# State-space weights prepared in the feed-forward block, full 128x128 output products, and attention steps that alternate with one step of other work

## The chip, the cores and the metric

The kernel runs on one core of a Trainium2 chip. The metric is the device time of one execution in microseconds (us), the median of several runs. The engines are TensorE (PE), VectorE (DVE), ScalarE (ACT), GpSimd (POOL) and SyncE (SP); SP only issues DMAs here. TensorE's granted clock is shown as a share of full speed: 1.00 is 2.4 GHz, 0.50 is 1.2 GHz.

## The reference

A sequence of 512 tokens of width 1024 goes through two layers of a first block (latent and differential attention) and then through two layers of a second block, to which the change belongs. A layer of the second block is a gated feed-forward block, a token mixer and another feed-forward block:

```
x = post_add(x, swiglu(pre(x, 0), ffn_w_in[l, 0], ffn_w_out[l, 0]), 0, 0.5)
y = token_mixer(pre(x, 1), ...)
x = post_add(x, y, 1, 1.0)
x = post_add(x, swiglu(pre(x, 2), ffn_w_in[l, 1], ffn_w_out[l, 1]), 2, 0.5)
```

The mixer projects its input to u, q, k, v, f and two gates, and computes

```
state[t] = lam_bar * state[t-1] + b_bar u[t]       (complex, 32 groups x 64 states)
y_ssm    = Re(C state) + d u                       (512 wide)
y_a      = z_val * sigmoid(z_gate),  z = gelu(y_ssm) @ glu_w
y_b      = forgetting_attention(q, k, v, f) @ attn_w_out      (causal, 8 heads)
out      = (sigmoid(g_a) y_a + sigmoid(g_b) y_b) @ w_out
```

lam_bar, b_bar and the powers of lam_bar depend on parameters alone, not on x.

## The kernel before, in words

Every large product is done as three matmuls on a high and a low part of both sides (`mm3`, L336 to L338; for products with tokens on the output's rows, `tokens`, L413 to L415). Weights stream in 512 KB units (`unit`): SP loads raw, ScalarE casts the high part (L319), VectorE subtracts to get the low part (L320); there are three buffers of each. A weight block (`mblock`) is 24 matmuls of 512 columns into one PSUM tile `acc`. The program is written in Python generators; a scheduler then puts the instructions in an order for each engine's queue, and each queue runs strictly in its order.

`ffn` works through 22 pairs of gate and up columns in chunks of SPLIT_K = 8, 7, 7. For a pair there are two weight blocks, then L1053 (tanh), L1054 and L1055 (products on VectorE), and a split into high and low (L425 on ScalarE, L428 on VectorE or GpSimd by turns). `pairs` opens a chunk's buffers by touching each on GpSimd (L396). After a chunk the four token tiles are multiplied with the chunk's output weights. Between, `pump` runs steps of the modulation (L999, one load and one VectorE operation each). After the first chunk of a layer's first feed-forward block, `ssm_params` computes lam_bar's powers.

`mixer` projects u and q, sends u through DRAM to get a layout by groups (four groups q of 128 channels), and runs three generators side by side: `ssm`, the attention (`fox_in`, `fox`), and the gated products. `side` interleaves them by the table MIX. For each q, `ssm` loads 256 KB of B and C, forms b_bar times powers on VectorE (`cplx`, L1223 to L1228), transposes it (L1248), forms C times powers and a rotation table on GpSimd (L1218 to L1263 and again L1223 to L1228), then the convolution kernel inside blocks of four tokens (L1278, L1281, masked at L1284), the inputs to the states (L1292), a scan on VectorE (L1303) and the outputs: four products of decreasing width (L1323) and 32 narrow ones with 32 weight columns (L1328), followed by a gelu. The attention's `fox` handles 8 heads; a head has scores for its query tiles (L575), masks, exponentials (L601), transposes (L584) and products with v (L1521).

Of the kernel before, what the change touches and what calls it, by code (L numbers as in the profile page):

```python
# [10 lines left out]
F32 = mybir.dt.float32  # L11
# [14 lines left out]
SPLIT_K = (8, 7, 7)  # L26
NH = 6
MIX = (1, 3, 1, 16)
# [5 lines left out]
BUFS = dict(raw=3, wh=3, wl=3, big=34, tmp=5, hf=3, ms=5, s16=8, pw=1, pr=1, acc=3, att=2, aux=2, yps=1, mod=2, sums=1)  # L34
# [114 lines left out]
def make_consts():  # L149
# [7 lines left out]
    c[:, C_BLK:C_BLK + 128] = (q // 32 == k // 32).astype(f)  # L157
# [79 lines left out]
class Net:  # L237
# [804 lines left out]
    def ffn(self, l, i, h, nxt, between):  # L1042
# [3 lines left out]
        for p, n in enumerate(SPLIT_K):  # L1046
# [24 lines left out]
            if p < len(SPLIT_K) - 1:  # L1071
                for t in range(4):
# [22 lines left out]
    def ssm_params(self, l):  # L1095
# [38 lines left out]
        v.scalar_tensor_tensor(ab, in0=th, scalar=-1.0, in1=th, op0=ALU.mult, op1=ALU.max)  # L1134

# [58 lines left out]
        v.tensor_tensor(wi, wi, d1, op=ALU.mult)  # L1194
        for j in range(3):
# [7 lines left out]
        return dict(rho=r[:, 3], tc=tc_, ts=ts_, l=(lr, li), f=(fr, fi))  # L1203

    def ssm(self, l, P, u, ud, out):

        nc = self.nc
        v, g = nc.vector, nc.gpsimd
        d4 = [128, 4, 4, 32]

        def v4(t):
            return t.rearrange("p (a b c) -> p a b c", a=4, b=4)

        def v3(t):
            return t.rearrange("p (a b) -> p a b", a=4)

        def mul(o, a, b):
            g.tensor_tensor(o, a, b, op=ALU.mult)  # L1218

        def cplx(e, o, a, b, c, d, view):  # L1220

            t = self.big()
            e.tensor_tensor(view(o[:, 0]), a, c, op=ALU.mult)  # L1223
            e.tensor_tensor(view(t[:, 0]), b, d, op=ALU.mult)
            e.tensor_tensor(o[:, 0], o[:, 0], t[:, 0], op=ALU.subtract)
            e.tensor_tensor(view(o[:, 1]), a, d, op=ALU.mult)
            e.tensor_tensor(view(t[:, 1]), b, c, op=ALU.mult)
            e.tensor_tensor(o[:, 1], o[:, 1], t[:, 1], op=ALU.add)  # L1228

        for q in range(4):  # L1230
            pq = slice(q * 4, q * 4 + 4)
            bk = self.big()
            bc, kt = v3(bk[:, 0]), v3(bk[:, 1])
            nc.sync.dma_start(bk[:, 0], self.io["ssmbc"][l, q])
            bl = self.big()
            b0, b1 = (v3(bk[:, 0])[:, c].rearrange("p (a b) -> p a b", a=4).unsqueeze(2).to_broadcast(d4)
                      for c in range(2))
            f0, f1 = (f[:, pq].unsqueeze(3).to_broadcast(d4) for f in P["f"])
            cplx(v, bl, b0, b1, f0, f1, v4)
            bb = self.tmp(256)  # L1240
            nc.scalar.copy(bb.rearrange("p (c a b) -> p c a b", c=2, a=4),
                           bl.rearrange("p c (a j b) -> p c a j b", a=4, j=4)[:, :, :, 3])
            gt = self.big()
# [9 lines left out]
            nc.scalar.mul(bc[:, 3], bc[:, 3], -1.0)  # L1253
            cl = self.big()
            cv = [bc[:, c].rearrange("p (a b) -> p a b", a=4).unsqueeze(1).to_broadcast(d4) for c in (2, 3)]
# [326 lines left out]
```

## Time and profile before

| | |
|---|---|
| median of 3 runs | 3258.07 us (3257.98 to 3263.37) |
| profiled execution | 3255.93 us, span 3254.2 us, granted clock 0.99 |
| TensorE busy | 97% of the span |
| VectorE, ScalarE, GpSimd busy | 59%, 37%, 16% |
| DMA | 385.8 MB, mean 119 GB/s |
| stages of the second block | 935, 1308, 1720, 2094, 2466, 2882 us to the end |

The stages were read from the stores of the residual at each stage's end: from 935 us the first feed-forward block of layer 0, then its mixer, its second feed-forward block, and the same three for layer 1. "Busy" counts instructions in work, not peak use; a matmul's recorded end is modelled and overlaps the next one's start, so that prices of matmuls are taken from distances between starts. Idle time of an engine is listed with the instruction whose end released it.

### The profile page before, as it was taken

To read this page: it belongs to the slowest core of one execution; us is meant where nothing else is said; L and a number is where in the kernel's file an instruction comes from. 1 tells how busy PE (TensorE), PEld (TensorE's weight loads), DVE (VectorE), ACT (ScalarE), POOL (GpSimd) and SP (SyncE) were. 2 spreads that over 40 slices of the span, in tenths; PEclk is the share of its full clock that TensorE was granted. 3 is DMA by queue.
4 is the path that set the end of the run, shared out by engine and by line. 5 is a ranking of instruction groups with operands and counts; after the bars stand their busy time and mean duration, and the time that the engine had idled before them with its cause. 6 is when DMAs were issued, how large, how long until landed. Compare 5 with 4: busy or idle time off the path is not lost. (4 is left out here: it accounts for less than half of the span.)

```text
span 3254.2 us, 42296 instructions
## 1 busy us (share of the span) xinstructions
PE 3150.2 (97%) x16138; PEld 2568.7 (79%) x16138; DVE 1932.3 (59%) x3517; ACT 1208.1 (37%) x2103; POOL 513.2 (16%) x580
## 2 busy tenths in 40 slices
PE   8999999999999999998999999999998989999999
PEld 8777878778788888876778888888888777788887
DVE  4787765787855847567565533634345676653334
ACT  3455433555332313334443222432234434442312
POOL 1200132000230101353001000100003340010000
PEclk9999999999999999999999999999999999999999
DMA  5242532243626537321233632332233221322313
GB/s 170 95 146 89 181 142 86 89 140 109 215 89 209 199 114 250 98 84 53 72 123 104 201 104 95 139 110 81 95 136 108 72 69 52 124 98 97 128 66 110
DMA packets 135514, 385.80 MB, mean 119 GB/s; under 512 B 15840, under 2 KB 22544, under 8 KB 135312
## 3 DMA queue, kind: packets, MB, share of 16 engines
q1 hardware_dynamic: 132208, 377.31, 34.3%
q0 software_dynamic: 1056, 3.17, 0.3%
q10 hardware_dynamic: 2048, 2.62, 0.3%
q8 instruction: 127, 2.08, 0.3%
q14 instruction: 75, 0.61, 0.1%
HBM read 361.52 MB, written 18.90 MB: 117 GB/s over the span
## 5 line engine op out<-in xcount | busy, mean ns | idle before, releaser
L336 PE MATMUL acc<-big,wh 128*128 128x512 f32 (+1 forms) x2744 | 1068.4, 390 | 13.2 <-DVE tmp L719 8.5
L337 PE MATMUL acc<-big,wh 128*128 128x512 f32 (+1 forms) x2744 | 1062.2, 387 | 0.7 <-POOL big L513 0.7
L338 PE MATMUL acc<-big,wl 128*128 128x512 f32 (+1 forms) x2744 | 1060.9, 387 | 0.0
L320 DVE TENSOR_TENSOR wl<-raw,wh 128x1024 fp32r<-128x1024 f32 x394 | 500.9, 1273 | 539.7 <-ACT wh L319 515.2
L319 ACT CAST wh<-raw 128x1024 fp32r<-128x1024 f32 x394 | 413.4, 1049 | 1001.2 <-PE acc L337 490.8
L336 PEld LDWEIGHTS acc<-big,wh 128*128 128x128 f32 x2744 | 520.1, 190 | 124.0 <-issue 10.2
L338 PEld LDWEIGHTS acc<-big,wl 128*128 128x128 f32 x2744 | 519.7, 189 | 106.4 <-issue 0.6
L337 PEld LDWEIGHTS acc<-big,wh 128*128 128x128 f32 x2744 | 520.5, 190 | 103.2 <-POOL big L513 1.2
L999 DVE SCALAR_TENSOR_TENSOR ms<-ms,big 128x512 f32<-128x512 f32 x288 | 198.7, 715 | 48.9 <-DMA ms<-in_modw_dram 48.4
L428 POOL TENSOR_TENSOR big<-tmp,big 128x512 fp32r<-128x512 f32 (+1 forms) x44 | 70.0, 1591 | 810.5 <-ACT big L425 810.5
L1055 DVE SCALAR_TENSOR_TENSOR tmp<-tmp,acc 128x512 f32<-128x512 f32 (+1 forms) x88 | 57.1, 649 | 150.5 <-PE acc L338 150.2
L425 ACT ACTIVATE big<-tmp 128x512 fp32r<-128x512 f32 (+1 forms) x148 | 88.0, 595 | 145.2 <-POOL tmp L875 58.0
L320 DVE TENSOR_TENSOR big<-raw,big 128x1024 fp32r<-128x1024 f32 x92 | 114.8, 1259 | 14.0 <-ACT big L319 14.0
L413 PE MATMUL acc<-big,big 128*128 128x512 f32 x288 | 112.9, 392 | 0.0
L415 PE MATMUL acc<-big,big 128*128 128x512 f32 x288 | 112.5, 391 | 0.0
L415 PE MATMUL att<-big,big 128*128 128x512 f32 x288 | 112.4, 390 | 0.0
L414 PE MATMUL acc<-big,big 128*128 128x512 f32 x288 | 112.4, 391 | 0.0
L413 PE MATMUL att<-big,big 128*128 128x512 f32 x288 | 112.2, 390 | 0.0
L414 PE MATMUL att<-big,big 128*128 128x512 f32 x288 | 112.2, 389 | 0.0
L319 ACT CAST big<-raw 128x1024 fp32r<-128x1024 f32 x92 | 94.7, 1042 | 43.7 <-DMA raw<-in_w_dram 43.7
L601 ACT ACTIVATE big<-att,sm 128x512 f32<-128x512 f32 (+2 forms) x112 | 69.5, 623 | 110.0 <-DVE sm L599 98.9
L584 PE MATMUL aux<-cst,big 128*128 128x128 f32 x512 | 95.3, 284 | 12.9 <-DVE big L589 5.5
(399 smaller groups left out, 5014.0 us busy)
## 6 DMA issues: line engine op xcount, KB each, us to landing
raw<-in_w_dram SPq DMA_DIRECT2D x486, 512.0 KB
ms<-in_modw_dram SPq DMA_DIRECT2D x288, 256.0 KB
xb2l0s<-big SPq DMA_DIRECT2D x12, 512.0 KB
big<-xb2l0s SPq DMA_DIRECT2D x12, 512.0 KB
xb1l<-big SPq DMA_DIRECT2D x8, 512.0 KB
big<-xb1l SPq DMA_DIRECT2D x8, 512.0 KB
xb2l1s<-big SPq DMA_DIRECT2D x8, 512.0 KB
big<-xb2l1s SPq DMA_DIRECT2D x8, 512.0 KB
```

What stands on the lines that cost most here:

```text
L319: nc.scalar.copy(hi[:, :n], raw[:, :n])
L320: nc.vector.tensor_tensor(lo[:, :n], raw[:, :n], hi[:, :n].bitcast(F32), op=ALU.subtract)
L336: nc.tensor.matmul(ps, lhsT=hi, rhs=a, start=first, stop=False)
L337: nc.tensor.matmul(ps, lhsT=hi, rhs=b, start=False, stop=False)
L338: nc.tensor.matmul(ps, lhsT=lo, rhs=a, start=False, stop=last)
L413: nc.tensor.matmul(ps[m], lhsT=a, rhs=hi, start=c == o[0], stop=False)
L414: nc.tensor.matmul(ps[m], lhsT=a, rhs=lo, start=False, stop=False)
L415: nc.tensor.matmul(ps[m], lhsT=b, rhs=hi, start=False, stop=c == o[-1])
L425: nc.scalar.activation(hi, src, AF.Copy, scale=scale)
L428: eng.tensor_tensor(lo, src, hi.bitcast(F32), op=ALU.subtract)
L584: nc.tensor.transpose(ps[:, j * 128:(j + 1) * 128], p[:, kc * 128:(kc + 1) * 128], self.ident)
L999: nc.vector.scalar_tensor_tensor(w, in0=w, scalar=0.5, in1=self.sc[m], op0=ALU.mult, op1=ALU.mult, accum_out=sums[:, n, m:m + 1])
```

## The change

A new generator `ssm_prep` does in a layer's first feed-forward block what depends on parameters alone. It is advanced by one step at each weight block and each output token tile. First come the parameters in five steps, then for each q the complex products, now all on VectorE (new L1229 to L1231, 18 operations a group), the transposes (new L1268), and the convolution kernel as 16 narrow products (new L1287, L1290). GpSimd's queue stores four 512 KB tiles for each q in DRAM (new L1235, L1304 to L1308; the zeros of the triangular tile too). This block's chunks become 5, 5, 5, 7, and it pumps half as many modulation steps; these run in later blocks instead. In the mixer, `ssm` loads the four tiles and u one group ahead on SP. The outputs are 128x128 products (new L1376, L1378) and go through DRAM on GpSimd's queue to get back to their layout. `side` and its table go; each of 24 attention steps is followed by one gate block or gated product (`fill`) and one state-space step. The first half of a head pair's q and k is split one pair ahead. There are three more `big` buffers and a smaller scratch for DMA descriptors.

```diff
-SPLIT_K = (8, 7, 7)
+SPLIT_K = ((5, 5, 5, 7), (8, 7, 7))
-MIX = (1, 3, 1, 16)
...
-    c[:, C_BLK:C_BLK + 128] = (q // 32 == k // 32).astype(f)
+    c[:, C_BLK:C_BLK + 128] = (q % 32 == k).astype(f)
...
+        prep = self.ssm_prep(l) if i == 0 else iter(())
+        for p, n in enumerate(SPLIT_K[i // 2]):
...
-                f(*[self.mblock(self.wk(f"in{i}"), h) for _ in range(2)], FULL)
+                pg = self.mblock(self.wk(f"in{i}"), h)
+                next(prep, None)
+                f(pg, self.mblock(self.wk(f"in{i}"), h), FULL)
                 self.pace = mid[j][:, 0, 0:1].bitcast(F32)
-                self.pump(2)
+                next(prep, None)
+                self.pump(1 if i == 0 else 2)
...
+                    next(prep, None)
             if p == 0:
                 gate = self.gate_row(l, i)
-                if i == 0:
-                    self.ssm_p = self.ssm_params(l)
+        for _ in prep:
+            pass
...
+    def ssm_prep(self, l):
 
         nc = self.nc
         v, g = nc.vector, nc.gpsimd
+        P = {}
+        for _ in self.ssm_params(l, P):
+            yield 1
...
+        def cplx(o, a, b, c, d, view, sign):
+
+            plus = (ALU.subtract, ALU.add)[::sign]
+            for k, x, y in ((0, c, d), (1, d, c)):
+                v.tensor_tensor(view(o[:, k]), a, x, op=ALU.mult)
+                v.tensor_tensor(view(t[:, k]), b, y, op=ALU.mult)
+                v.tensor_tensor(o[:, k], o[:, k], t[:, k], op=plus[k])
+                yield 1
+
+        def store(i, o, eng=g):
+            eng.dma_start(ssd[q, i], o.rearrange("p a b -> p (a b)"))
...
+            for _ in cplx(cl, l0, l1, c0, c1, lambda x: x.rearrange("p (a b c) -> p a b c", a=4, b=4), -1):
+                yield 1
+            store(1, cl)
...
+            it = cplx(cs, *ta, *tb, lambda x: x.rearrange("p (a b c) -> p a b c", a=4, b=8), 1)
+            yield next(it)
+            for i in range(4):
+                s = slice(i * 32, i * 32 + 32)
+                for c in range(2):
+                    w = bb[:, c * 128 + i * 32:c * 128 + i * 32 + 32]
+                    nc.tensor.matmul(ps[s, 0:32], lhsT=w, rhs=bc[:, 2 + c, s], start=c == 0, stop=c == 1)
+                for c in range(2):
+                    w = bb[:, c * 128 + i * 32:c * 128 + i * 32 + 32]
+                    nc.tensor.matmul(ps[s, 32:128], lhsT=w, rhs=cl[:, c, i * 128:i * 128 + 96],
+                                     start=c == 0, stop=c == 1)
+            nc.scalar.copy(bk[:, 1, 0:128], ps[:, 0:128])
+            yield next(it)
+            store(2, cs)
...
+            tri = ssd[q, 3, :, 0:512].rearrange("p (i x) -> p i x", i=4)
+            for j in range(4):
+                js = slice(j * 32, j * 32 + 32)
+                g.dma_start(tri[js, :, j * 32:].rearrange("e i x -> i e x"), bk[:, 1, 0:128 - j * 32])
+                if j:
+                    g.dma_start(tri[js, :, 0:j * 32], 
+                                self.cst[js, C_BLK + 32:C_BLK + 32 + j * 32].unsqueeze(1).to_broadcast([32, 4, j * 32]))
+            g.dma_start(ssd[q, 3, :, 512:1024], ru[:, 0])
...
+        def load(q):
+
+            ts = [self.big() for _ in range(4)]
+            for i, t in enumerate(ts):
+                nc.sync.dma_start(t.rearrange("p a b -> p (a b)"), self.ssd[l][q, i])
+            uu = self.big()
+            nc.sync.dma_start(uu[:, 1], ud[q])
+            return *ts, uu
...
+            if q < 3:
+                ahead = load(q + 1)
+            yield 1
-            uq = u[q // 2][:, q % 2]
-            for a in range(4):
-                n = (4 - a) * 128
-                nc.tensor.matmul(y_ps[:, a * 128:], lhsT=kt[:, a], rhs=uq[:, :n], start=a == 0, stop=False)
-            for j in range(4):
-                o = y_ps[:, j * 128:(j + 1) * 128]
+            for i in range(4):
+                s = slice(i * 128, (i + 1) * 128)
+                nc.tensor.matmul(y_ps[:, s], lhsT=kr[:, 0, s], rhs=uu[:, 1, s], start=True, stop=False)
                 for c in range(2):
-                    for i in range(4):
-                        nc.tensor.matmul(o[i * 32:(i + 1) * 32], lhsT=cl[:, c, j * 128 + i * 32:j * 128 + i * 32 + 32],
-                                         rhs=hh[:, c, i * 128:(i + 1) * 128], start=False, stop=j == 3 and c == 1)
+                    nc.tensor.matmul(y_ps[:, s], lhsT=cl[:, c, s], rhs=hh[:, c, s], start=False, stop=c == 1)
...
+            g.dma_start(yd[q], q2)
+            d = yd[q].rearrange("(j e) (i k) -> j e i k", j=4, i=4)
+            for i in range(4):
+                g.dma_start(uu[i * 32:(i + 1) * 32, 0].rearrange("e (j k) -> e j k", j=4),
+                            d[:, :, i].rearrange("j e k -> e j k"))
+            yield 1
+            out.append(self.split(uu[:, 0].rearrange("p (j k) -> p k j", j=4), scale=0.5, view="p (k j) -> p k j"))
...
+        def fill():
+
+
+            for j in range(8):
+                t = self.big()
+                tg.append(t)
+                for k in range(2):
+                    ps = self.mblock(self.wk("gate"), h)
+                    nc.scalar.activation(t[:, k], ps, AF.Tanh, scale=0.5)
+                    yield 1
+            for _ in S_:
+                pass
...
-        n = 0
-        for it in (self.fox_in(l, h, st), self.fox(st, yb)):
-            for _ in it:
-                side(n)
-                n += 1
-        for _ in S_:
-            pass
+        for n, _ in enumerate(self.fox_in(l, h, st)):
+            next(S_, None)
+        for n, _ in enumerate(self.fox(st, yb)):
+            next(F_, None)
+            next(S_, None)
...
-                    if q == 2:
-                        yield 1
+                    if q and e and hp < 3:
+                        n = hp + 1
+                        ahead = self.halves_qk(qf[n // 2][:, n % 2], kf[n // 2][:, n % 2])
+                    yield 1
...
-    nc = bacc.Bacc("TRN2", target_bir_lowering=False, num_devices=1)
+    nc = bacc.Bacc("TRN2", target_bir_lowering=False, num_devices=1, dynamic_dma_scratch_size=2048)
```

On VectorE, the first mixer of the kernel before, where the weights of one group are formed (`wl` and `raw` are streamed weights, `pw` the powers, `aux` a PSUM tile):

```order
L1223 TENSOR_TENSOR big_12252<-big_12250,pw_9881 128x512
L1224 TENSOR_TENSOR big_12253<-big_12250,pw_9881 128x512
L1226 TENSOR_TENSOR big_12252<-big_12250,pw_9881 128x512
L1225 TENSOR_TENSOR big_12252<-big_12252,big_12253 128x512
L1227 TENSOR_TENSOR big_12253<-big_12250,pw_9881 128x512
L320 TENSOR_TENSOR wl_12449<-raw_12446,wh_12448 128x1024
L1228 TENSOR_TENSOR big_12252<-big_12252,big_12253 128x512
L1252 COPY big_12262<-aux_12263 128x512
```

And in the changed kernel on VectorE, in the middle of the first feed-forward block (L319 is the low part of a weight, L998 a modulation step, L1054 and L1055 the pair's products):

```order
L1229 TENSOR_TENSOR big_9946<-big_9944,pw_9318 128x512
L1230 TENSOR_TENSOR big_9441<-big_9944,pw_9318 128x512
L1230 TENSOR_TENSOR big_9441<-big_9185,big_9944 128x512
L1231 TENSOR_TENSOR big_9946<-big_9946,big_9441 128x512
L998 SCALAR_TENSOR_TENSOR ms_10609,sums_8179<-ms_10609,big_276 128x512
L1229 TENSOR_TENSOR big_10031<-big_9185,big_9944 128x512 x2
L319 TENSOR_TENSOR wl_9909<-raw_9906,wh_9908 128x1024
L1054 SCALAR_TENSOR_TENSOR tmp_9830<-tmp_9829,acc_9769 128x512
L1231 TENSOR_TENSOR big_10031<-big_10031,big_9441 128x512
L1230 TENSOR_TENSOR big_9441<-big_9185,big_9944 128x512
L1230 TENSOR_TENSOR big_9441<-big_9185 128x512
L1231 TENSOR_TENSOR big_10031<-big_10031,big_9441 128x512
```

The complex products have left the mixer's queue and stand one or two at a time between the low parts of weights and the pairs' products of the feed-forward block.

On GpSimd, around the opening of a later chunk in the first feed-forward block before (L396 opens buffers, L428 is the low part of a pair, L995 paces the modulation's loads, L470 belongs to norms):

```order
L428 TENSOR_TENSOR big_9923<-tmp_10410,big_9923 128x512 [waits Activation_49,Pool_49]
L396 CAST big_10763<-ones 128x1 [waits PE_49]
L396 CAST big_10764<-ones 128x1 [waits PE_49,Pool_49]
L396 CAST big_10765<-ones 128x1 [waits DVE_49,PE_49]
L428 TENSOR_TENSOR big_10760<-tmp_10917,big_10760 128x512 [waits Activation_49]
L995 COPY ms_11013<-big_10761 128x1 [waits Activation_49]
L995 COPY ms_11015<-big_10761 128x1
L995 COPY ms_11017<-big_10761 128x1
```

And in the changed kernel on GpSimd, from the first group's stores on (L395 opens buffers, L1022 and L1023 fetch the gate's row):

```order
L1300 MEMSET big_9531 128x4 [waits Activation_49]
L1308 DMA ssd_9440<-big_9531 128x512 [waits DMASW0_49,Pool_49]
L1235 DMA ssd_9440<-big_9534 128x1024 [waits DMASW1_49,DVE_49]
L1022 DMA gates_86<-tmp_9583 8x128 [waits DMASW2_49,Activation_49]
L1023 DMA big_9581<-gates_86 128x1024 [waits DMAHW5_49,DMASW3_49,DMASW2_49]
L395 CAST big_9588<-ones 128x1 [waits PE_49]
L395 CAST big_9589<-ones 128x1 [waits DMAHW0_49,PE_49]
L395 CAST big_9590<-ones 128x1 [waits PE_49]
L395 CAST big_9591<-ones 128x1 [waits PE_49]
L395 CAST big_9592<-ones 128x1 [waits PE_49]
L1235 DMA ssd_9440<-big_9705 128x1024 [waits DMASW4_49,DVE_49,Activation_49]
L1300 MEMSET big_10028 128x4 [waits PE_49,Activation_49]
```

Stores of the prepared tiles, which wait for VectorE, now stand ahead of the touches that open the next chunk's buffers.

On TensorE, the outputs of one group in the first mixer, before (`yps` and `aux` are PSUM tiles, L917 and the new L916 belong to the attention's inputs):

```order
L338 MATMUL acc_12846<-big_8577,wl_12843 128x512
L1323 MATMUL yps_12880<-big_11733,big_12630 128x512
L1323 MATMUL yps_12880<-big_11733,big_12630 128x384
L917 MATMUL aux_12873<-cst,tmp_12871 128x128 x4
L1323 MATMUL yps_12880<-big_11733,big_12630 128x256
L1323 MATMUL yps_12880<-big_11733,big_12630 128x128
L1328 MATMUL yps_12880<-big_12832,big_12656 32x128 x32
L336 MATMUL acc_12933<-big_8571,wh_12929 128x512
```

And in the changed kernel:

```order
L337 MATMUL acc_12959<-big_8577,wl_12956 128x512
L1376 MATMUL yps_12993<-big_12655,big_12650 128x128
L1378 MATMUL yps_12993<-big_12895,big_12648 128x128 x2
L1376 MATMUL yps_12993<-big_12655,big_12650 128x128
L1378 MATMUL yps_12993<-big_12895,big_12648 128x128 x2
L1376 MATMUL yps_12993<-big_12655,big_12650 128x128
L916 MATMUL aux_12986<-cst,tmp_12984 128x128 x4
L1378 MATMUL yps_12993<-big_12895,big_12648 128x128 x2
L1376 MATMUL yps_12993<-big_12655,big_12650 128x128
L1378 MATMUL yps_12993<-big_12895,big_12648 128x128 x2
L574 MATMUL att_13021<-big_12881,big_12880 128x128
```

The 4 wide and 32 narrow products of a group have become 12 of 128x128, with attention scores (new L574) right behind.

## Rows read from the trace of the kernel before

**Rows 1.** The page, part 1: busy us, share of the span, instructions.

```profile
PE 3150.2 (97%) x16138; PEld 2568.7 (79%) x16138; DVE 1932.3 (59%) x3517; ACT 1208.1 (37%) x2103; POOL 513.2 (16%) x580
```

**Rows 2.** Busy time by stage: stretch, its us, five engines, clock, DMA share, GB/s.

```profile
935.00:1308.00 373.00, 370.21 (x1735) 306.72 (x1736) 241.56 (x575) 118.86 (x171) 41.83 (x62) 1.00 0.53 182
1308.00:1720.00 412.00, 387.34 (x2309) 311.25 (x2308) 263.45 (x389) 170.93 (x325) 110.58 (x109) 0.98 0.25 86
1720.00:2094.00 374.00, 373.05 (x1774) 309.94 (x1773) 173.26 (x269) 115.76 (x167) 34.85 (x60) 1.00 0.38 129
2094.00:2466.00 372.00, 371.24 (x1760) 308.27 (x1760) 163.97 (x318) 118.92 (x177) 31.45 (x39) 1.00 0.32 107
2466.00:2882.00 416.00, 388.84 (x2299) 311.87 (x2298) 264.38 (x383) 169.98 (x322) 112.51 (x109) 0.98 0.26 85
```

**Rows 3.** TensorE's groups in the first mixer (1308 to 1720): busy, mean | idle before.

```profile
L584 PE MATMUL aux<-cst,big 128*128 128x128 f32 x64 | 13.5, 289 | 3.3 <-ACT big L587 1.5 <-DVE big L589 1.5 <-DVE big L1510 0.3
L575 PE MATMUL att<-big,big 128*128 128x128 f32 (+3 forms) x32 | 11.7, 372 | 4.6 <-ACT big L601 4.6
L1281 PE MATMUL aux<-big,tmp 128*128 128x384 f32 x16 | 7.5, 588 | 3.1 <-POOL big L1263 1.9 <-POOL big L1260 1.3
L1248 PE MATMUL aux<-cst,big 128*128 128x128 f32 x32 | 6.0, 319 | 10.6 <-DVE big L1228 5.6 <-DVE big L1225 3.1 <-ACT big L922 1.9
```

**Rows 4.** The same in the second mixer (2466 to 2882).

```profile
L584 PE MATMUL aux<-cst,big 128*128 128x128 f32 x64 | 13.7, 290 | 4.0 <-DVE big L589 2.3 <-ACT big L587 1.4 <-DVE big L1510 0.3
L575 PE MATMUL att<-big,big 128*128 128x128 f32 (+3 forms) x32 | 11.6, 369 | 4.4 <-ACT big L601 4.3
L1248 PE MATMUL aux<-cst,big 128*128 128x128 f32 x32 | 5.9, 313 | 14.6 <-DVE big L1228 7.1 <-DVE big L1225 5.7 <-ACT big L922 1.9
```

**Rows 5.** Busy time around one of the mixer's stops, columns as in rows 2.

```profile
1350.00:1356.70 6.70, 3.79 (x31) 3.34 (x29) 6.70 (x5) 2.59 (x3) 6.70 (x6) 1.00 0.00 1
1356.70:1363.50 6.80, 4.30 (x12) 2.78 (x12) 4.66 (x4) 1.51 (x3) 6.80 (x5) 0.50 0.44 133
```

**Rows 6.** Timeline of TensorE in the first mixer: start, us, instruction.

```profile
1385.41 0.39 PE L336 MATMUL acc<-big,wh 128*128 128x512 f32 x1
1385.64 0.39 PE L337 MATMUL acc<-big,wh 128*128 128x512 f32 x1
...
1386.11 2.32 PE L1323 MATMUL yps<-big,big 128*128 128x512 f32 x8
1388.35 1.95 PE L1328 MATMUL yps<-big,big 128*32 128x128 f32 x64
1390.24 0.50 PE L336 MATMUL acc<-big,wh 128*128 128x512 f32 x1
...
1367.24 2.05 PE L1292 MATMUL att<-big,big 128*128 128x128 f32 x16
1369.05 0.48 PE L336 MATMUL acc<-big,wh 128*128 128x512 f32 x1
...
1419.15 1.46 PE L1281 MATMUL aux<-big,tmp 128*128 128x384 f32 x4
1420.44 1.73 PE L1292 MATMUL att<-big,big 128*128 128x128 f32 x14
```

**Rows 7.** DMA issues of GpSimd's queue: count, KB each, median us to landing.

```profile
big<-gates POOLq DMA_DIRECT2D x6, 512.0 KB, 4.2
...
gates<-tmp POOLq DMA_DIRECT2D x6, 4.0 KB, 1.7
```

**Rows 8.** Timeline of VectorE in the first mixer, one complex product's start.

```profile
1348.84 0.69 DVE L1223 TENSOR_TENSOR big<-big,pw 128x512 f32<-128x512 f32 x1 [4.27 <-DMA big<-in_ssmbc_dram]
1349.45 1.56 DVE L1224 TENSOR_TENSOR big<-big,pw 128x512 f32<-128x512 f32 x1
```

**Rows 9.** VectorE's groups in the first feed-forward block (935 to 1308).

```profile
L999 DVE SCALAR_TENSOR_TENSOR ms<-ms,big 128x512 f32<-128x512 f32 x108 | 77.3, 748 | 31.2 <-DMA ms<-in_modw_dram 30.9
...
L1055 DVE SCALAR_TENSOR_TENSOR tmp<-tmp,acc 128x512 f32<-128x512 f32 (+1 forms) x22 | 14.2, 647 | 14.6 <-PE acc L338 14.5
```

More of the change, by code (lines that the diff above doesn't have):

```diff
@@ L1269, in ssm @@
-            ct, st = cs[:, 0], cs[:, 1]
-            ru = self.big()
-            rho = v3(ru[:, 0])
+            store(0, gt)
+            yield 1
+            yield 1
+            cs = self.big()
+            ta = [x[:, pq, 16:24].unsqueeze(3).to_broadcast(s4) for x in (P["tc"], P["ts"])]
+            tb = [x[:, pq, 0:16].unsqueeze(2).to_broadcast(s4) for x in (P["tc"], P["ts"])]
+            it = cplx(cs, *ta, *tb, lambda x: x.rearrange("p (a b c) -> p a b c", a=4, b=8), 1)
+            yield next(it)
@@ L1273, in ssm @@
             g.memset(rho[:, :, 0:1], 0.0)
-            nc.sync.dma_start(ru[:, 1], ud[q])
-            yield 1
-            ps = self.t("aux", [128, 512])
-            for c in range(2):
-                nc.tensor.matmul(ps[:, 0:128], lhsT=bb[:, c * 128:(c + 1) * 128], rhs=bc[:, 2 + c],
-                                 start=c == 0, stop=c == 1)
-            for c in range(2):
-                nc.tensor.matmul(ps[:, 128:512], lhsT=bb[:, c * 128:(c + 1) * 128], rhs=cl[:, c, 0:384],
-                                 start=c == 0, stop=c == 1)
@@ new lines, in ssm_prep, with ssm, v3, mul @@
+            g.dma_start(ssd[q, 3, :, 512:1024], ru[:, 0])
+            yield 1
+    def ssm(self, l, ud, out):
+        nc = self.nc
+        v, g = nc.vector, nc.gpsimd
+        yd = self.dr.tile([4, 128, 512], F32, name=f"yd{l}")
+        def v3(t):
+            return t.rearrange("p (a b) -> p a b", a=4)
+        def mul(o, a, b):
+            g.tensor_tensor(o, a, b, op=ALU.mult)
+        def load(q):
[5 more added lines that the diff above has]
+            return *ts, uu
+        ahead = load(0)
+        for q in range(4):
+            gt, cl, cs, kr, uu = ahead
+            ct, st = cs[:, 0], cs[:, 1]
+            yield 1
@@ L1291, in ssm @@
                     s = slice(i * 128, (i + 1) * 128)
-                    nc.tensor.matmul(ps[:, s], lhsT=gt[:, c, s], rhs=ru[:, 1, s], start=True, stop=True)
+                    nc.tensor.matmul(ps[:, s], lhsT=gt[:, c, s], rhs=uu[:, 1, s], start=True, stop=True)
                 sp.append(ps)
@@ L1377, in gated @@
                 yield 1
-        def side(i):
-            while side.s * MIX[0] < i + 1 and next(S_, None):
-                side.s += 1
-            while len(tg) < 8 and len(tg) * MIX[1] < i + 1:
-                tg.append(self.g_pair(h))
-            while len(gl) == 4 and side.g < len(tg) and side.g * MIX[2] < i + 1 - MIX[3] and next(G_, None):
-                side.g += 1
-        side.s = side.g = 0
-        S_ = self.ssm(l, P, u, ud, gl)
-        G_ = gated()
-        next(S_)
-        n = 0
-        for it in (self.fox_in(l, h, st), self.fox(st, yb)):
-            for _ in it:
-                side(n)
-                n += 1
-        for _ in S_:
-            pass
-        for _ in G_:
+        S_ = self.ssm(l, ud, gl)
+        F_ = fill()
+        next(S_)
+        for n, _ in enumerate(self.fox_in(l, h, st)):
[3 more added lines that the diff above has]
+            next(S_, None)
+        for _ in F_:
             pass
@@ L1413, in mixer @@
         return self.stage(f"b2l{l}s1", self.rows("mo", 8), mg, lambda t, ps: self.add(t, ps, gate), nxt)
-    def g_pair(self, h):
-        t = self.big()
-        for k in range(2):
-            ps = self.mblock(self.wk("gate"), h)
-            self.nc.scalar.activation(t[:, k], ps, AF.Tanh, scale=0.5)
-        return t
     def fox_in(self, l, h, st):
@@ L1487, in fox @@
         qf, kf, vf = st["q"], st["k"], st["v"]
+        ahead = st["qk"]
         for hp in range(4):
-            qk = self.halves_qk(qf[hp // 2][:, hp % 2], kf[hp // 2][:, hp % 2])
+            qk = ahead
             for e in range(2):
```

83 lines of the change are left out of this document (34 added, 49 removed).

## The prediction

> **What bounds the kernel now.** I read the page's first part, then the busy time by stage, then the groups of matmuls inside the mixers with the idle time ahead of them, then the order of single instructions around the state-space work. TensorE is busy 3150.2 of 3254.2 us [rows 1]: in most of the program nothing but a shorter list of matmuls could help. The table by stage says where that is not so [rows 2]. The first feed-forward block of a layer (935 to 1308 us, and 2094 to 2466) leaves TensorE idle for 2.8 and 0.8 us. The two mixers (1308 to 1720, 2466 to 2882) leave it idle for 24.7 and 27.2 us, and there the granted clock means 0.98, against 1.00 in the feed-forward blocks. So the mixer has slack and the feed-forward block has none: work that only VectorE and GpSimd do can be moved into the latter, where VectorE is busy 241.6 of 373 us and 164.0 of 372.
>
> In the mixers the idle time has two sources. Ahead of the transposes L1248 and the products L1281 TensorE sat for 10.6 and 3.1 us in layer 0 and for 14.6 us in layer 1, released mostly by VectorE's complex products and GpSimd's: preparation of weights [rows 3, 4]. Ahead of the attention's scores and transposes (L575, L584) it sat for 4.6 + 3.3 and 4.4 + 4.0 us, released by the softmax. And after a stretch with such stops, TensorE busy 3.79 of 6.70 us, the clock stands at 0.50 for 6.8 us: the lower level, 1.2 GHz [rows 5]. (Lines from L1229 on in what follows that are said to be new, and L395 and L427, are lines of the changed kernel; all others are lines of the kernel before.)
>
> **TensorE work taken out of the mixers** (sum of both layers, eight groups q; a matmul of plain 32-bit floats leaves two records, and I count records by distance of starts, since their ends overlap). Sixteen records of 128x128 go from 1367.24 to 1369.05, 0.113 us each [rows 6]. So the 64 transposes cost 7.2 us and the 32 records of L1278 3.6 us; the 32 of L1281 cost (1420.44 − 1419.15)/4 = 0.323 each, 10.3 us; L1323 takes 1388.35 − 1386.11 = 2.24 us a group, 17.9 us; the 64 narrow records of L1328 take 1390.24 − 1388.35 = 1.89 us a group, 15.1 us. Sum 54.1 us. What comes instead is, per group, 4 triangular products (L1376) and 8 state products (L1378) of 128x128, 24 records: 8 x 24 x 0.113 = 21.7 us. The mixers lose **32.4 us** of matmuls.
>
> **TensorE work put into the feed-forward blocks.** The transposes come back, 7.2 us. The kernel products become 16 a group with 32 weight columns and 32 or 96 data columns, 256 records. The nearest row is L1328, also 32 weight columns, 1.89/64 = 0.030 us; the other end is a full product's 0.113. That gives 7.6 to 28.9 us. I take 0.06, 15.4 us, since successive products here add into the same 32 rows of the output, where L1328's went round four; half are also shorter. Sum **22.6 us** (15 to 36). The Trainium skill (TensorE: Matmul & The Clock Gate, Part 3) says that products with different 32-row outputs run side by side in the array, and by that rule the new order, two and two in one place, would not; it speaks against this part of the change. With its reading the new products would cost the upper end, 28.9, and the total would come out 13.5 us worse; the trace shows the rotating case alone.
>
> **Idle time in the mixers.** The waits on preparation, 10.6 + 3.1 + 14.6 = 28.3 us, lose their cause: the weights arrive by four loads a group, issued a whole group ahead. The attention's 16.3 us are met by one weight block (24 matmuls 0.23 us apart, as the pair at 1385.41 [rows 6]: 5.5 us) between every two steps, longer than the longest single wait there; I take 12.7 of them. The other 7.2 us I leave. **41 us** (28.3 to 51.8). New there: the outputs go through DRAM (one store, four gathers, a split). A store to DRAM and the gather of it on GpSimd's queue are seen to land in 1.7 and 4.2 us [rows 7]; the gated products that read the result stand two attention steps behind the last group, over 10 us, so I cost it at nothing; without that cover it is some 7 us a layer, once. The transfers add 4 x 2.25 MB a layer on SP's queue, where DMA is busy a quarter of the mixer [rows 2].
>
> **Clock.** Means of 0.98 over 412 and 416 us are 2% of full speed lost, 16.6 us, of which TensorE, busy 4.30 of 6.80 us of such a stretch [rows 5], feels some 10. I take **12 us** (8 to 16), because restarts after a stop go too.
>
> **VectorE and GpSimd in the feed-forward block.** Added per layer: 72 operations on 128x512. In the mixer the same operation took 0.69 us as GpSimd began and 1.56 us alongside it [rows 5, 8] (GpSimd is busy all of 6.70 us there). I take 0.68 (49.0 us), as the GpSimd half of these products is gone and what GpSimd keeps there is 41.8 us busy in 373 [rows 2]; at 1.56 it would be 112 us. The Trainium skill (SBUF — State Buffer, Who interferes with whom) states that VectorE with two SBUF inputs and a GpSimd operation that reads SBUF lock each other out; by it only overlap with GpSimd's 41.8 us counts, and the rows agree. Four copies out of PSUM and eight more partial sums at 0.69 add 8.2; 30 fewer modulation steps at 0.72 [rows 9] take away 21.5. VectorE in layer 0: 241.6 + 49.0 + 8.2 − 21.5 = 277 of about 384 us, 72%: no bound by itself. The 30 steps fall to the last feed-forward block of layer 0, where TensorE was busy 373.05 of 374 us and VectorE only 173.3 [rows 2].
>
> With chunks of five instead of eight, the first output matmuls of a chunk need its last pair after 24 matmuls, 5.5 us; the chain behind it (L1054 and L1055, 0.65 each [rows 9], a cast and a subtraction of about as much) is some 2.5 us. Covered, unless VectorE is late; there is one boundary more. GpSimd's queue gets nine stores a group, each behind the VectorE operation that it stores; behind them stand L395, which opens the next chunk's buffers, and L427, half of the low parts. The 24 zero stores stand at the very start, outside all this. I put **5 us** for all such waits (0 to 30).
>
> **Sum:** −32.4 − 41 − 12 + 22.6 + 5 = −57.8 us on the profiled execution's 3255.93; the median of the runs, 3258.07, is 2.1 above it. On the median: **3200 us**. About 0.2% (6.5 us) is what a measurement of this kernel can tell from no change.
>
> **Rivals.**
> *Waits move rather than go.* VectorE late in the feed-forward block (operations at 1.56 us wherever GpSimd works, modulation steps that wait for their weights ahead of a low part), or the attention still waits because its scores and the state-space products share two PSUM buffers. For it: VectorE's margin falls from a third to a quarter, with queues in fixed order. Against: TensorE has up to three weight blocks in hand. Price: the 12.7 of the attention stay, 15 us more in the feed-forward blocks and the narrow products at their upper end: 57.8 − 12.7 − 15 − 13.5 = 17 gained, at worst; half of that is the middle, 37 gained: about 3221.
> *All of it goes.* Idle 51.8, clock 16, narrow products at 0.030, no new waits: 32.4 + 51.8 + 16 − 14.8 = 85 us, 3173.
> *Slower: GpSimd's queue becomes the bound of the feed-forward block.* Nine stores a group, run one behind another's landing at 4.2 us [rows 7], hold the queue 38 us a group; the feed-forward block has some 85 us for a group, but L395 and L427 stand behind the stores and TensorE waits for both. For it: a store's descriptors get a smaller scratch after the change, and the queue never carried more than two transfers in a row. Against: the order shows several stores in flight (each waits for the transfer some eight places earlier), and pairs are written well ahead. It decides from 57.8/8 = 7.2 us of stall a group; at 10 us the total is 22 us slower, 3280.
> *The change does not do what it says*: the order shows no complex product left in the mixer, so 0.01.
>
> **Chances.** Forecast's neighbourhood (3183 to 3212) 0.50; all of it goes 0.13; waits move (3212 to 3251) 0.24; within 0.2% of no change 0.04; slower 0.09. Faster is 0.50 + 0.13 + 0.24 = 0.87. The range runs from 3170, just past the best case, to 3245, just past the worst of the moved waits; outside it lie the 0.13 of no gain and loss, and a little at either end.
>
> **What would show it.** In the profile of the changed kernel: mixers of about 370 us each instead of 412 and 416, clock 1.00 there, idle time below 8 us each, a 24-record group of L1376 and L1378 in 2.7 us; first feed-forward blocks longer by 11 to 15 us, with L1287 and L1290 near 0.06 us a record and VectorE's L1229 to L1231 at 0.68 us. Wrong, if TensorE's idle time in the first feed-forward blocks exceeds 10 us (released by L395, L427 or a low part of weights), or if in the mixer waits for loads from the state-space store or for the two shared PSUM buffers replace the old ones.

## The result, and the profile after

The changed kernel takes 3215.65 us (median; 3213.36 to 3220.3), against 3258.45 for the kernel before with its runs beside it. The ratio is 0.9867, 95% interval 0.9855 to 0.9878: 42.8 us faster where 58 were forecast. The time lies inside the stated range, 16 us above the forecast; that is some 4 us above what the prediction called the forecast's neighbourhood (3183 to 3212), in the stretch that it gave to "waits move".

The page's first part and the busy time by stage (columns as in [rows 1] and [rows 2]; the bounds are again the residual's stores):

```profile
PE 3128.0 (97%) x15946; PEld 2566.8 (80%) x15946; DVE 1952.6 (61%) x3623; ACT 1209.9 (38%) x2111; POOL 447.9 (14%) x610
```

```profile
938.50:1325.00 386.50, 380.65 (x1896) 313.02 (x1897) 268.59 (x596) 125.35 (x191) 60.84 (x93) 1.00 0.52 175
1325.00:1702.00 377.00, 364.93 (x2043) 303.18 (x2042) 220.22 (x348) 163.56 (x306) 53.37 (x76) 0.98 0.34 118
1702.00:2077.40 375.40, 374.22 (x1781) 310.67 (x1780) 196.58 (x343) 117.06 (x172) 36.78 (x62) 1.00 0.45 154
2077.40:2463.00 385.60, 382.52 (x1916) 315.44 (x1915) 219.68 (x407) 125.53 (x193) 49.28 (x78) 1.00 0.37 126
2463.00:2841.00 378.00, 364.05 (x2046) 302.39 (x2045) 220.28 (x348) 163.75 (x308) 53.55 (x76) 0.99 0.34 118
```

Against [rows 2] the two mixers fell from 411 to 377.0 and from 416 to 378.0 us (the first mixer's last store stands at 1719.15 us, which [rows 2] rounds up to 1720), and the two first feed-forward blocks grew from 373 to 386.5 and from 372 to 385.6, by the times of the stores themselves by 13.1 and 14.5 us. The second feed-forward block of layer 0 stayed at 375 us. The first block of the program (up to 935 us), which the change does not touch, ended 3.8 us later in this execution; that is within what one measurement can tell (6.5 us). So the feed-forward terms together (22.6 + 5 us in the sum) were right to a microsecond, and the 13 us that are missing are missing in the mixers: they gave 72 us, not 85. There TensorE's idle time went from 24.7 and 27.2 us to 12.1 and 13.9 (stretch minus busy), and the granted clock is still 0.98 and 0.99.

What TensorE waited for in the first mixer (us in total, times, longest; one line of 0.2 us left out):

```profile
PE att L574 <- ACT big L600: 4.0, 2, 2.0
PE aux L1504 <- DVE tmp L1499: 3.1, 1, 3.1
PE aux L916 <- ACT tmp L913: 2.2, 1, 2.2
PE att L336 <- POOL big L512: 1.4, 2, 0.8
PE acc L335 <- ACT big L318: 0.6, 1, 0.6
PE aux L583 <- DVE big L1558: 0.5, 2, 0.2
```

None of these is a wait on prepared weights; [rows 3] had 13.7 us of those. Two are new: the forget gates' prefix product (L1504) and the transpose of v (L916). The scores' wait (L574) is not; the kernel before had nearly the same sum, in six smaller stops:

```profile
PE att L575 <- ACT big L601: 4.6, 6, 2.0
```

The second mixer has the same lines (4.2, 3.1 and 2.5 us) and 1.9 us at L583. The timeline of the stop at L1504 shows what such a stop costs, and the busy time behind it (columns as in [rows 2]) the granted clock:

```profile
1381.74 0.40 PE L335 MATMUL acc<-big,wh 128*128 128x512 f32 x1
1385.26 0.59 PE L1504 MATMUL aux<-tmp,cst 128*128 128x1 f32 x2 [3.12 <-DVE tmp L1499]
1385.71 0.78 PE L336 MATMUL acc<-big,wh 128*128 128x512 f32 x1
1386.29 0.63 PE L337 MATMUL acc<-big,wl 128*128 128x512 f32 x1
1386.71 0.63 PE L335 MATMUL acc<-big,wh 128*128 128x512 f32 x1
```

```profile
1384.40:1391.10 6.70, 5.84 (x15) 4.68 (x16) 4.74 (x10) 4.31 (x14) 0.00 (x0) 0.50 0.54 191
```

TensorE stands for 3.12 us, and the matmuls behind it start 0.42 us apart, not 0.23: the granted clock fell to 0.50, the lower level, around this stop and stayed there for 6.8 us.

### The profile page after: what moved, and what is told of

It is laid out like the page before. It is cut to its first block, busy times and chain, and to the rows that moved or that the text cites. A ratio compares the mean times of both kernels' runs of the same rounds, so it can differ in the third digit from the quotient of the medians.

```text
span 3213.7 us, 42239 instructions
## 1 busy us (share of the span) xinstructions
PE 3128.0 (97%) x15946; PEld 2566.8 (80%) x15946; DVE 1952.6 (61%) x3623; ACT 1209.9 (38%) x2111; POOL 447.9 (14%) x610
## 5 line engine op out<-in xcount | busy, mean ns | idle before, releaser
L319 DVE TENSOR_TENSOR wl<-raw,wh 128x1024 fp32r<-128x1024 f32 x400 | 499.8, 1252 | 525.3 <-ACT wh L318 510.0
L998 DVE SCALAR_TENSOR_TENSOR ms<-ms,big 128x512 f32<-128x512 f32 x288 | 194.2, 701 | 36.2 <-DMA ms<-in_modw_dram 35.7
L427 POOL TENSOR_TENSOR big<-tmp,big 128x512 fp32r<-128x512 f32 (+1 forms) x42 | 68.4, 1628 | 676.6 <-ACT big L424 676.6
L1055 DVE SCALAR_TENSOR_TENSOR tmp<-tmp,acc 128x512 f32<-128x512 f32 (+1 forms) x88 | 57.2, 651 | 149.5 <-PE acc L337 149.2
L319 DVE TENSOR_TENSOR big<-raw,big 128x1024 fp32r<-128x1024 f32 x86 | 109.5, 1283 | 17.3 <-ACT big L318 17.0
L412 PE MATMUL acc<-big,big 128*128 128x512 f32 x264 | 104.0, 394 | 0.0
L413 PE MATMUL acc<-big,big 128*128 128x512 f32 x264 | 103.7, 393 | 0.0
L414 PE MATMUL acc<-big,big 128*128 128x512 f32 x264 | 103.7, 393 | 0.0
L583 PE MATMUL aux<-cst,big 128*128 128x128 f32 x512 | 94.5, 281 | 9.5 <-DVE big L828 4.6
L597 DVE TENSOR_REDUCE sm<-att 128x1 f32<-128x512 f32 (+3 forms) x150 | 88.4, 596 | 24.4 <-PE att L1551 22.5
L412 PE MATMUL att<-big,big 128*128 128x512 f32 x264 | 103.2, 391 | 0.0
L414 PE MATMUL att<-big,big 128*128 128x512 f32 x264 | 103.1, 390 | 0.0
L413 PE MATMUL att<-big,big 128*128 128x512 f32 x264 | 102.9, 390 | 0.0
```

What stands on the lines that cost most here:

```text
L319: nc.vector.tensor_tensor(lo[:, :n], raw[:, :n], hi[:, :n].bitcast(F32), op=ALU.subtract)
L412: nc.tensor.matmul(ps[m], lhsT=a, rhs=hi, start=c == o[0], stop=False)
L413: nc.tensor.matmul(ps[m], lhsT=a, rhs=lo, start=False, stop=False)
L414: nc.tensor.matmul(ps[m], lhsT=b, rhs=hi, start=False, stop=c == o[-1])
L583: nc.tensor.transpose(ps[:, j * 128:(j + 1) * 128], p[:, kc * 128:(kc + 1) * 128], self.ident)
L597: nc.vector.tensor_reduce(m[:, j:j + 1], s_ps[j], axis=AX.X, op=ALU.max)
```

## The experiments

All twelve kernels are the changed kernel with the edits that are shown or named. They ran in three groups of four, in the order below, and the kernel before ran beside each group (3258.03, 3259.53 and 3259.39 us); ratios are to it. The changed kernel itself, the base, ran again in the first group only. Stages are compared with those of the changed kernel's profile above.

**The base again** (no edit).

> The changed kernel once more, as the base of the runs beside it. 3216 us, within 4 us, with the same six stops of TensorE in the mixers (two at the scores, one at the forget gates' prefix product, one at the first transpose of v, in each).

3216.66 us, ratio 0.9869 (0.9854 to 0.9884). The base moved by one microsecond between two measurements; a single stage moved by up to 2 us (the first feed-forward block of layer 0 took 388.5 us between its stores, against 386.6).

**Gate blocks ahead of the forget gates' product.**

```diff
         for n, _ in enumerate(self.fox_in(l, h, st)):
+            if n == 0:
+                next(F_, None)
+                next(F_, None)
             next(S_, None)
```

> Two gate blocks are taken from the attention's steps and put between the forget gates' matmuls and the prefix product that waits for VectorE's chain. Theory A (the gain that is missing sits in stops that the new interleaving made, and in the clock falls behind them): the stop of 3.1 us a mixer goes and so does the clock fall at it, 6 to 11 us less, 3205 to 3210. Theory B (the mixer is bound by its list of matmuls, and a stop that is taken away at one place comes back at another): within 3 us of 3216.

3203.62 us, ratio 0.9831 (0.9816 to 0.9846): 13 us less, theory A. No wait at L1504 is listed any more, and the mixers are 4.5 and 5 us shorter; what the median has beyond these 9.5 us lies in stages that the edit does not touch:

```profile
1325.20:1697.70 372.50, 362.67 (x2044) 301.10 (x2043) 221.60 (x347) 163.27 (x307) 55.11 (x76) 0.99 0.35 120
2456.30:2829.30 373.00, 362.71 (x2043) 301.22 (x2042) 221.03 (x347) 163.46 (x306) 55.19 (x76) 0.99 0.35 119
```

**v's transposes one block later.**

```diff
+        pv = self.mblock(self.wk("v"), h)
         for j in range(4):
-            self.to_tokens(self.mblock(self.wk("v"), h), st["v"], j)
+            p, pv = pv, self.mblock(self.wk("v"), h) if j < 3 else None
+            self.to_tokens(p, st["v"], j)
```

> The transposes of v are put one weight block later, so that the copy that they read has 5.5 us. Theory A: the stops of 2.2 and 2.5 us go, with their clock fall 4 to 8 us less, 3208 to 3212. Theory B: within 3 us of 3216.

3209.42 us, ratio 0.9849 (0.9835 to 0.9864): 7 us less, though the interval touches the base's. In the profile the mixers are 1.4 and 2.9 us shorter; that much is the edit's, the rest of the 7 may be spread. In the first mixer v's wait of 2.2 us is gone, but the waits at L583 have grown from 0.5 to 2.0 us and one of 1.0 us at L1378 is new: part of the stop moved.

**Scans one step later.**

```diff
+            yield 1
             v.tensor_tensor_scan(zr, kr[:, 1], zr, 0.0, op0=ALU.mult, op1=ALU.add)
```

> One more step in the state-space generator, ahead of its two scans, so that the scans stand behind the next softmax's maxima on VectorE and not ahead of them, and the weight block between two score steps is whole again. Theory A: the two stops of 2 us a mixer at the scores go, with their clock falls 8 to 13 us less, 3203 to 3208. Theory B: the state-space chain ends later, and what was won comes back as a wait of the outputs or of the gated products: within 3 us of 3216.

3211.86 us, ratio 0.9858 (0.9842 to 0.9875), not to be told from the base. The mixers took 377.6 and 377.4 us, as before. The waits say why. One of the two stops at the scores went in each mixer (L574 is down to 2.1 us), and this line, the gated products' wait for the last group's output, is new in each:

```profile
PE acc L335 <- ACT big L424: 2.2, 1, 2.2
```

That is theory B in this place.

**The three together.**

> The three moves of the runs before together. Theory A (stops and their clock falls are what is missing): their gains add, 20 to 32 us less than the changed kernel, 3184 to 3196, idle time of TensorE below 5 us a mixer and granted clock 1.00 there. Theory B (bound by the list of matmuls): 3210 or more.

3209.22 us, ratio 0.9844 (0.983 to 0.9857): 7 us less than the base, but 6 us more than the first of the three alone; its four runs lie 8 us apart. The expectation that gains add fell. The second mixer's longest waits say why:

```profile
PE acc L335 <- ACT big L424: 4.5, 2, 4.3
PE aux L583 <- ACT big L586: 3.2, 1, 3.2
PE att L574 <- ACT big L600: 2.1, 1, 2.1
...
```

The gated products wait 4.3 us for the last group's output (the first mixer has 4.2). With the scan step alone this wait was 2.2 us, with the gate blocks' edit alone 0.2. The state-space chain had become four steps longer and the gate blocks ran out two steps earlier, so the work that covered the outputs' way through DRAM was spent. This is the cover of which the prediction said "some 7 us a layer, once" if it went.

**The old interleaving.** The preparation and the new outputs stay; `side`, its table, and the `fox` of the kernel before come back:

```diff
...
-        for n, _ in enumerate(self.fox_in(l, h, st)):
-            next(S_, None)
-        for n, _ in enumerate(self.fox(st, yb)):
-            next(F_, None)
-            next(S_, None)
...
+        for it in (self.fox_in(l, h, st), self.fox(st, yb)):
+            for _ in it:
+                side(n)
+                n += 1
...
```

> The preparation and the new outputs stay, but the mixer's interleaving is the one of the kernel before: the table-driven one, two gate blocks at a time, four yields per head pair and no splitting ahead. If the interleaving carries the attention's part of the gain, as the prediction has it (12.7 of 16.3 us of waits and most of the clock): 3230 to 3245. If moving the preparation alone carries it: 3216 or less, and the new interleaving is worth nothing.

3219.05 us, ratio 0.9873 (0.986 to 0.9887): 2 to 3 us above the base, whose interval it overlaps. The mixers:

```profile
1323.20:1704.50 381.30, 365.62 (x2044) 299.55 (x2043) 221.43 (x347) 163.38 (x306) 53.24 (x76) 0.99 0.34 117
2463.00:2843.60 380.60, 365.85 (x2044) 299.92 (x2043) 221.67 (x348) 163.42 (x307) 53.18 (x76) 0.99 0.34 117
```

```profile
PE aux L584 <- DVE big L589: 4.8, 3, 2.1
PE att L575 <- ACT big L601: 2.8, 5, 0.7
PE acc L336 <- ACT big L425: 2.3, 2, 1.8
PE yps L1379 <- DVE big L1367: 2.2, 1, 2.2
...
```

So the preparation and the outputs bring the mixers from 411 and 416 us to 381.3 and 380.6, and the new interleaving takes off a further 4.3 and 2.6. No run takes the preparation and the outputs apart; their shares are priced by rows alone. The list of the first mixer's waits (its longest lines, numbered one higher than in the changed kernel) has neither the forget gates' product nor v's transpose: those two stops came with the new interleaving. Other places stop TensorE instead, for 15.7 us in sum against 12.1.

**Chunks of 8, 7, 7.**

```diff
-SPLIT_K = ((5, 5, 5, 7), (8, 7, 7))
+SPLIT_K = ((8, 7, 7), (8, 7, 7))
```

> Chunks of 8, 7, 7 in the layers' first feed-forward blocks, as before. If the shorter chunks cost something at their boundaries (one more in each block, the rival's waits on VectorE): 3 to 6 us less, 3210 to 3213. If they are free: within 3 us of 3216. If they were needed to free buffers for the preparation: slower, 3220 or more, with waits for buffers.

3207.84 us, ratio 0.984 (0.9827 to 0.9854): 8 us less. The first feed-forward block of layer 0 is 3.8 us shorter, layer 1's 1.9:

```profile
937.70:1320.50 382.80, 379.65 (x1898) 313.39 (x1897) 267.48 (x587) 126.50 (x192) 57.23 (x95) 1.00 0.52 177
```

The changed kernel's waits in that block had this line, which is gone here (as it is in the next run, with chunks of five, so that it is not the whole of the difference):

```profile
PE acc L337 <- DVE wl L319: 2.7, 2, 1.4
```

The block took 384.6 to 388.5 us between its stores in all nine profiled kernels with chunks of five, and 382.5 to 383.2 in the three with 8, 7, 7 and the halved modulation.

**Modulation as before.**

```diff
-                self.pump(1 if i == 0 else 2)
+                self.pump(2)
```

> Twice the modulation steps per pair in the first feed-forward blocks, as before the change: some 30 operations of 0.72 us more for VectorE in each. If VectorE has margin there (prediction: 72% busy): within 3 us of 3216. If it is near its bound, low parts of weights come late: 10 us or more slower, with TensorE waiting for L319.

3209.55 us, ratio 0.9844 (0.983 to 0.9857). VectorE is busy 292.94 of 384.6 us, and TensorE waits 0.6 us for a low part of weights (L413). It is not slower, and I read nothing into the 7 us, since the stages differ by 2 us at most; the medians of the other single edits, 7 and 8 us, are worth no more than their stages show either.

```profile
936.70:1321.30 384.60, 380.77 (x1899) 313.48 (x1898) 292.94 (x668) 126.84 (x192) 58.06 (x99) 1.00 0.59 200
```

**What paid, together:** the first two edits and the chunks.

> The two moves that paid by themselves (gate blocks ahead of the forget gates' product, transposes of v one block later) with chunks of 8, 7, 7 in the first feed-forward blocks. If their gains add (13, 7 and 9 us by the medians before; by the stage times of the profiles 9.4, 4.2 and 5.7): 3190 to 3200. If stops only move, as the three moves together showed: 3205 or more.

3193.52 us, ratio 0.9801 (0.9788 to 0.9815): 22 us below the changed kernel. By the medians the three edits alone gave 28 us, so medians do not add; by the stages that they touch they gave 19.3, and here the two mixers and the two first feed-forward blocks are together 19.9 us shorter. So by stages the gains add. None of the edits takes away the cover of the last group's outputs: the gated products' wait for them is 0.2 us in each mixer. Three of the four stages:

```profile
935.70:1318.90 383.20, 379.77 (x1898) 313.35 (x1898) 266.54 (x587) 126.30 (x192) 58.22 (x94) 1.00 0.53 176
1318.90:1690.10 371.20, 362.63 (x2044) 301.17 (x2043) 221.23 (x347) 163.19 (x307) 55.10 (x76) 0.99 0.35 120
2447.30:2818.00 370.70, 361.12 (x2044) 300.39 (x2043) 221.15 (x348) 163.46 (x307) 55.20 (x76) 1.00 0.35 120
```

**The scans again, with the chain's length kept.**

```diff
+            yield 1
             v.tensor_tensor_scan(zr, kr[:, 1], zr, 0.0, op0=ALU.mult, op1=ALU.add)
...
             if q < 3:
                 ahead = load(q + 1)
-            yield 1
```

> The same, and the two scans stand behind the next softmax's maxima, without making the state-space chain longer: the empty step behind the loads is taken out in exchange, so that the last group's outputs come as early as before and the gated products need not wait for them. If the 4 us of stop at the scores that were left in each mixer come from VectorE's order alone: 8 to 12 us less than the run beside it, idle time below 7 us a mixer. If they come from the two PSUM buffers or from ScalarE's queue: within 3 us of it.

3193.95 us, ratio 0.9803 (0.979 to 0.9817): the same, and the two stops of 2 us at the scores are still there. VectorE's timeline ahead of one of them (TensorE stands 2.04 us and resumes at 1469.02) shows that the edit failed at what it was for:

```profile
1463.45 2.29 DVE L1354 TENSOR_TENSOR_SCAN big<-big,big 128x512 f32<-128x512 f32 x1 [0.28 <-POOL big L1351]
1465.66 0.26 DVE L597 TENSOR_REDUCE sm<-att 128x1 f32<-128x128 f32 x1
1465.85 1.21 DVE L1355 TENSOR_TENSOR_SCAN big<-big,big 128x512 f32<-128x512 f32 x1
1466.98 0.39 DVE L597 TENSOR_REDUCE sm<-att 128x1 f32<-128x256 f32 x1
1467.41 1.06 DVE L598 TENSOR_SCALAR sm<-sm 128x2 f32<-128x2 f32 x1
```

The scheduler put the scans ahead of the softmax's maxima (L597) all the same. The run does not separate VectorE's order from the two shared PSUM buffers; what the rows show is that the maxima, whose scores were issued by 1463.7, ended at 1467.4, behind 3.5 us of scans, and that the exponentials that free the scores' buffers come after them.

**Outputs twice.**

```diff
-            for i in range(4):
+            for i in [*range(4)] * 2:
                 s = slice(i * 128, (i + 1) * 128)
                 nc.tensor.matmul(y_ps[:, s], lhsT=kr[:, 0, s], rhs=uu[:, 1, s], start=True, stop=False)
```

> Every output product of the state-space part is issued twice (the second time it overwrites), 192 records more in the program; everything else is the changed kernel. If the mixer is bound by its list of matmuls, as the sum of the prediction takes it: 8 groups x 24 x 0.113 = 21.7 us slower, 3238. If they lie beside other work (12 to 14 us of idle time are left in each mixer): under 10 us slower.

3235.09 us, ratio 0.9924 (0.991 to 0.9937): 18 to 19 us slower, and the mixers 11.1 and 9.8 us longer:

```profile
1324.50:1712.60 388.10, 375.11 (x2141) 313.09 (x2140) 220.35 (x348) 163.75 (x307) 53.36 (x76) 0.99 0.33 115
2474.50:2862.30 387.80, 374.57 (x2140) 313.09 (x2139) 220.39 (x348) 163.66 (x307) 53.57 (x76) 0.99 0.33 115
```

The 192 added records cost 20.9 us in the mixers, 0.109 each, which is their full spacing, even with 12 to 14 us of idle time beside them (13.0 and 13.2 us here): the idle time sits in stops that this work did not fill.

**Modulation as before, on top of what paid.**

> The first run of this call with the modulation steps as before the change as well (two per pair). If the margin on VectorE is real: within 3 us of the first run, or a little better since the steps leave the second feed-forward block. If the gain of 7 us seen with the steps alone is more than spread between runs: 5 to 7 us less than the first run.

3204.72 us, ratio 0.9836 (0.9822 to 0.9849): 11 us slower than the first run of its group. Neither expectation held. The first feed-forward block of layer 0 is 10.5 us longer than in that run, and TensorE waits for both parts of the weights (two of the lines):

```profile
936.70:1330.40 393.70, 384.00 (x1897) 314.95 (x1897) 289.11 (x659) 126.51 (x192) 64.07 (x99) 0.99 0.58 196
```

```profile
PE acc L413 <- DVE wl L319: 3.3, 3, 2.1
...
PE acc L412 <- ACT wh L318: 1.8, 2, 1.2
```

VectorE is no busier than with the chunks of five (289.11 us against 292.94), and there the same steps cost nothing. So the busy share alone does not tell the margin. That it depends on where the steps stand is my reading; no run shows it by itself.

## Why the prediction was right or wrong

**Matmuls: right, a little low.** The records of the triangular and state products start 0.11 us apart, the narrow ones in the feed-forward block take 1.03 us for 32 records:

```profile
1394.99 0.61 PE L1378 MATMUL yps<-big,big 128*128 128x128 f32 x4
1395.43 0.39 PE L1376 MATMUL yps<-big,big 128*128 128x128 f32 x2
1395.66 0.61 PE L1378 MATMUL yps<-big,big 128*128 128x128 f32 x4
...
1057.20 0.31 PE L1287 MATMUL aux<-big,big 128*32 128x32 f32 x4
1057.35 0.25 PE L1290 MATMUL aux<-big,big 128*32 128x96 f32 x1
1057.36 0.25 PE L1287 MATMUL aux<-big,big 128*32 128x32 f32 x2
1057.43 0.25 PE L1290 MATMUL aux<-big,big 128*32 128x96 f32 x1
...
1058.23 0.50 PE L335 MATMUL acc<-big,wh 128*128 128x512 f32 x1
```

That is 0.032 us a narrow record, 8.2 us in all, where I took 15.4 between two ends: the nearest row that I had, L1328's 0.030, was the price itself. The rows say why. The program issues four records of L1287 and four of L1290 for one quarter of the output's rows before it goes to the next quarter; but the next quarter's L1287 start (1057.36) when the first quarter has begun one of its L1290 (1057.35). What I wrote ahead of the prediction, that each queue runs strictly in its order, does not hold for the starts of these records. The quarters run side by side, as the Trainium skill's rule has it (TensorE: Matmul & The Clock Gate, Part 3); my reading, that two and two in one place would prevent it, was wrong, and so were the 28.9 us drawn from it. Doubling the output products cost 18 to 21 us against 21.7 computed: the price of a matmul in the mixer is its spacing, as the sum had it.

What was low is the price of the matmuls that went. Taken from start to start in both traces, without idle time, L1248, L1278, L1281, L1323 and L1328 took 59.6 us in the two mixers before, and L1376 and L1378 20.9 us after: 38.7 us out, where I had 32.4. I had priced them from a few rows at full clock; L1248, which stood behind most of the stops, took 8.4 us, not 7.2, and L1281 11.9, not 10.3.

**VectorE in the feed-forward block: right.** The 72 operations of a layer ran at the duration taken (49.9 us in layer 0, where I had 49.0), not at the 1.56 us of [rows 8]; single ones of L1229 took up to 1.78 us. A third of them:

```profile
L1231 DVE TENSOR_TENSOR big<-big,big 128x512 f32<-128x512 f32 x24 | 16.3, 685 | 0.0
```

VectorE was busy 268.59 of 386.5 us, 69%, where I had 72. The feed-forward blocks grew by 13.1 and 14.5 us against 13.8 forecast. Two errors cancelled in that, which is luck: the narrow products were cheaper by 3.6 us a block, and what is left of the growth when the transposes (7.2 us) and the narrow products (8.2) are taken off is 12.2 us, where I had put 5 for all waits. The chunks of five are 3.8 and 1.9 us of it; the rest is not taken apart. And 72% was no proof of margin: with chunks of 8, 7, 7 and the modulation as before VectorE was busy 73% of the block, and the block lost 10.5 us.

**Idle time in the mixers: the step that failed.** I let 41 of 51.8 us go; 25.8 went. The waits on preparation left as forecast (28.3 us); the other 23.5 became 26.0. I had counted 12.7 of the attention's 16.3 as met by the weight block between steps; 5.7 went, almost all of it at the transposes (7.3 to 2.4 us), while the scores kept 8.2 of 9.0 us. And I had counted as if covering old waits made no new ones. The runs show that it does: blocks that `side` had put behind the forget gates went to the attention, and their chain (3.1 us a mixer) and v's copy (2.2 and 2.5 us) stood bare. With the old interleaving back the mixers are 6.9 us longer and the kernel is 2 to 3 us slower, no more. This is the rival "waits move rather than go", by the first term of its price, the 12.7 us; its prices for the feed-forward block and for the narrow products did not come. Whether the scores' stops come from the two shared PSUM buffers, as that rival has it, or from VectorE's order stays open.

**Clock: the second step that failed.** I let 12 us go with the stops. But the stretches at the lower clock sum to 23.9 us in the two mixers (13.7 and 10.2), where they had been 34.1 (13.7 and 20.5): half of that is lost, 11.9 us where it had been 17.1, so that at most 5 us came. Of the eight stops of about 2 us or more in the two mixers of the trace (1.97 to 3.12), six have a low stretch that begins within 1.5 us of the stop's end. In the kernel with the three edits that paid, the means are 0.99 and 1.00.

That the mixers are only 13 us short, with 15 us of idle time and 7 of clock not gained, is luck too: TensorE's busy time there fell by 47.2 us (22.4 and 24.8 by [rows 2] and the table above), where matmuls and clock together had been put at 44.4, because the old matmuls were dearer than their prices in the sum.

**GpSimd's queue: right.** No matmul in the first feed-forward blocks waited for L395 or L427; the stores behind VectorE hold nothing up. The rival on the other side has nothing for it here.

## What to carry to other kernels

When waits are moved out of a stage, list which instructions covered what before, and name the chain that loses its cover; a wait is gone only when the next latest thing is earlier. Price matmuls added to a stage with idle time at their full spacing, unless they are put into the stops themselves, as the gate blocks were. And of edits that are put together, ask whether one takes away the cover of another: three that did not (9.4, 4.2 and 5.7 us by their stages) added up to 19.9 us, while the scan step, worth nothing alone, cost the gate blocks' edit some of its gain. Read such gains from the stages that an edit touches; one edit's median fell by 7 us where no stage fell by more than 2.

## What the runs showed of the hardware

Records of narrow products started out of the program's order where their outputs lie in different quarters of the rows: 32 records, issued quarter after quarter, took 1.03 us, 0.032 each, against 0.11 us for each record of a 128x128 product. And at six of eight stops of only 2 to 3 us, in a TensorE that was otherwise busy, a stretch at the lower clock began within 1.5 us of the stop's end (matmuls 0.42 us apart where 0.23 is usual).
